# One hybrid decoder layer on one core: branch A's key low parts stored twice per head, so that both score products of branches A and B contract over 128 rows

## The chip, the cores and the metric

The kernel runs on one core of one Trainium2 chip. The metric is device time in microseconds. Three runs of the kernel before took 2040.52, 2048.73 and 2062.89 us; their median is 2048.73. One more execution was recorded by the hardware profiler, and all rows below come from it.

## The reference, cut to what matters

One layer of a decoder with 1024 tokens and 1024 channels: a token mixer of three branches, then a convolutional FFN. All branches read one projection of the normed input. Branch A is dilated sliding-window attention with three (window, dilation) groups of four heads, combined by their softmax denominators. Branch B is grouped-query attention in a window of 128, with sinks. Branch C is stick-breaking attention. A head has 64 channels. The scores of A and B come from blocks of 128 queries against their own block of keys and the one before:

```python
def banded_attention(q, k, v, bias, mask):
    ...
    logits = jnp.einsum('nkgbqd,nkbsd->nkgbqs', qb, kw, preferred_element_type=jnp.float32) * SCALE
    logits = jnp.where(mask, logits + bias[:, :, None], -jnp.inf)
    m = jnp.max(logits, axis=-1)
    p = jnp.exp(logits - m[..., None])
    l = jnp.sum(p, axis=-1)
    num = jnp.einsum('nkgbqs,nkbsd->nkgbqd', p, vw.astype(jnp.float32))
```

The branches' outputs are projected, gated and summed, and an output projection follows. Everything is float32.

## The kernel before, in words

**Precision.** A float32 operand is cut into a high part (type fp32r, which one pass of TensorE carries) and a low part, the rest (`split`, lines 116 to 122). A product is then high by high, high by low and low by high. The large projections are formed from seven half-size products each (`Strassen`); their products are lines 137 and 1333.

**Stages in time.** The pre-norm and the input projections of 27 pairs of column tiles come first, up to about 580 us. Attention of branches A and B follows, up to about 829 us. Then branch C runs with the gated projections of A and B as filler, then C's projection and the output projection, and from about 1130 us the FFN.

**How queries and keys are kept.** After each pair of column tiles `keep_qk` (lines 505 to 534) writes queries and keys to DRAM from a staging tile `hst`, by DMAs on GpSimd's queue. A column tile of 128 channels is two heads. In `q_d` each head has a tile of 128 rows: its high parts on its own 64 rows, its low parts on the other 64. In `k_d` there are four tiles of 128 rows per pair of heads: the high parts of each head, written twice (once on each half of the rows), and the low parts. For branch B and C the low parts of each head are also written twice. For branch A's six key tiles they are written once, both heads under each other, into tile 2 (lines 529 to 531).

**The score products.** `mm_qk` (line 714) forms the scores of one head for one block of queries with two products into the same PSUM columns. Line 717 contracts over all 128 rows: high by high on one half, low queries by high keys on the other. Line 719 adds high queries by low keys and contracts over the 64 rows of that head alone (`r`, rows 0 to 63 for head 0 and 64 to 127 for head 1). Branches A and B both use it. Branch C has its own two products (line 735), both over 128 rows, with key tiles `k` and `kl` per head.

**A step of A or B** (`att_AB`) takes two blocks of 128 queries and two heads. `scores`: eight products into two PSUM tiles `z_ab`, in columns of 128 (own block only) or 256; VectorE adds the bias and finds the row maxima (line 823); ScalarE takes the exponentials (lines 884 and 974; for B also a scaling, line 983). `transposed`: up to eight transposes of the weights on TensorE (line 841, `ps_pT`), copied out by VectorE (line 843). `values`: 128 by 64 products (line 851, `o_ab`). The scores of the next step are issued before the transposes of this one. Branch A has six units (two pairs of heads times three groups, in the order of dilation 4, 16, 1) of four steps each; branch B has four pairs of heads of four steps. One step of A and one of B alternate; B ends after 16 steps and A goes on alone for the last 8.

**Buffers and queues.** SyncE issues the loads, in order. Even units of A have their queries, keys and low keys in pool `ua`, odd ones in a shared tile `HA` and a tile `kl` of pool `ub`; a unit is loaded while the one before it runs. Branch B's values `b_v` have a tile of their own in `ua`; once B is done, the same place takes the low parts of branch C's second head (`c_kl`, two loads). Weights pass through the pool `wa`, tag `raw`, with two buffers. The order on each engine is made by the framework's scheduler from the program's order.

```python
    def mm_qk(z, hh, st, mv, low, ss, ms):
        q, k, kl, r = *low, HR[hh]
        nc.tensor.matmul(z, st[hh][:, ss], mv[hh][:, ms], start=True, stop=False)
        a, b = (q[hh], kl) if st is q else (kl, q[hh])
        nc.tensor.matmul(z, a[r, ss], b[r, ms], start=False, stop=True)
```

Of the kernel before, what the change touches and what calls it, by code (L numbers as in the profile page):

```python
# [18 lines left out]
P = 128  # L19
# [53 lines left out]
def decoder_kernel(ctx, tc, x, rel_bias, attn_pre, w_in, b_gate, sinks, w_br_a, w_br_b, w_br_c,  # L73
# [7 lines left out]
    # Left of SBUF: const, mbuf, hbuf, then what a phase needs; right: wa, b0.  # L81
# [23 lines left out]
    def dram_bc(v):  # L105
        """A row vector in DRAM, read by all partitions."""
        return bass.AP(v.tensor, v.offset, [[0, P], [1, v.shape[-1]]])
# [8 lines left out]
    def split(hi, lo, src, scale=1.0):  # L116
        """src * scale as hi + lo, hi with the bits that one pass of the tensor engine carries."""
# [12 lines left out]
    # float32 products in three passes over exact high and low parts  # L130
# [18 lines left out]
    # Both operands are cut in two along every dimension and the product is formed from seven half-size ones:  # L149
    # S1=A21+A22 S2=S1-A11 S3=A11-A21 S4=A12-S2; T1=B12-B11 T2=B22-T1 T3=B22-B12 T4=B21-T2  # L150
    # P1=A11.B11 P2=A12.B21 P3=S4.B22 P4=A22.T4 P5=S1.T1 P6=S2.T2 P7=S3.T3
    # C11=P1+P2 C12=P1+P6+P5+P3 C21=P1+P6+P7+P4 C22=P1+P6+P7+P5
    # A: the first column tile's channels are the upper rows, the second's the lower. B: channel half, token half.
# [47 lines left out]
    class Strassen:  # L201
# [53 lines left out]
        def products_begin(self, f, ug, uv):  # L255
            """The products in the order in which the operands come; neither needs ug and uv at first."""
# [40 lines left out]
    def operand_build(S, hfs, ks, cols):  # L297
        """Makers of T1, B22 with T2 and T3, and T4 from the halves of h, for the tiles ks and tokens cols; in place of h."""
# [42 lines left out]
    # pairs of column tiles of w_in: queries and keys, values, gates  # L341
# [66 lines left out]
    # Order of the work: n: pre-norm of a token tile; b, c: B11 and B21 of a channel tile (c: from PSUM at once);  # L408
    # x: a channel tile of the second half; t, u, v: T1, then B22 with T2 and T3, then T4 (T, U, V: on the other engine);
    # f: a step of P1 and P2 of a pair; w: weights of the next pair; r: the first pair's other operands.  # L410
# [41 lines left out]
    def init_vectors():  # L452
# [5 lines left out]
        # per-channel vectors, channels on partitions  # L458
# [13 lines left out]
        # bias by distance, reversed, masked distances at NEG; a copy per query row in DRAM  # L472
# [22 lines left out]
    def by_residue(t, dil):  # L495
        """Columns in natural token order, read in residue-major order: token dil * l + r at r * (1024 / dil) + l."""
        return t.rearrange("p (l r) -> p r l", r=dil)
# [7 lines left out]
    def keep_qk(c, u, r):  # L505
# [22 lines left out]
        for part in range(2):  # L528
            if part == 1 and KA <= c < KA + 6:
                nc.gpsimd.dma_start(dst[2], b[:, 1])  # L530
                continue
# [53 lines left out]
    def load_q(dst, c, cols=slice(0, T), eng=nc.sync, which=None):  # L585
        """Two heads' queries: a head's high parts at its rows, low parts at the other's."""
# [3 lines left out]
    def load_k(dst, c, which, cols=slice(0, T), eng=nc.sync):  # L590
        """Keys, high parts twice per head, then low parts."""
        eng.dma_start(dst.bitcast(F32), k_d[KS.index(c), which, :, cols].rearrange("h p t -> p h t"))

    def unit_tiles(odd):
        if odd:
            t = mbuf.tile([P, 4, T], F32R, tag="HA", name="qk")
            q, k, kl = t[:, 0:2], t[:, 2:4], ub.tile([P, 1, T], F32R, tag="kl", name="kl")
        else:
            q = ua.tile([P, 2, T], F32R, tag="q", name="q")
            k3 = ua.tile([P, 3, T], F32R, tag="k", name="k")  # L600
            k, kl = k3[:, 0:2], k3[:, 2:3]
        return dict(k3=None if odd else k3, q=q, k=k, kl=kl, v=(ub if odd else ua).tile([P, NB, P], F32, tag="v", name="v"))
# [4 lines left out]
    def load_A(n):  # L607
# [6 lines left out]
        load_k(u["kl"], KA + 2 * g + p, slice(2, 3))  # L614
        nc.sync.dma_start(u["v"], v_d[VS.index(VA + 2 * g + p)])
        u.update(q=per_head(u["q"]), k=per_head(u["k"]), kl=u["kl"][:, 0])
# [5 lines left out]
    def load_B_qk(p, cols=slice(0, T)):  # L622
        """Both heads of a pair share a key head."""
        if p == 0:
            t = mbuf.tile([P, 4, T], F32R, tag="HD", name="b_qk")
            uB.update(qk=t, q=per_head(t), k=[t[:, 2], t[:, 2]], kl=t[:, 3])
# [7 lines left out]
    def load_C(p, n, t):  # L634
        """Half n of a pair's tokens into t."""
        for hh in range(2):
            load_q(t["q"][hh].unsqueeze(1), QC + p, tok(n), which=hh)
            for i, x in enumerate(("k", "kl")):
                if t[x][hh] is not None:
                    load_k(t[x][hh].unsqueeze(1), KC + p, slice(2 * i + hh, 2 * i + hh + 1), tok(n))  # L640
# [3 lines left out]
    def first_C():  # L644
        u = unit_tiles(0)
        for n in range(2):
            load_q(u["q"][:, :, tok(n)], QC, tok(n))
            load_k(u["k3"][:, :, tok(n)], KC, slice(0, 3), tok(n))
            nc.sync.dma_start(u["v"][:, 4 * n : 4 * n + 4], v_d[VS.index(VC), :, 4 * n : 4 * n + 4])
            uC.setdefault(0, []).append(dict(q=[u["q"][:, hh, tok(n)] for hh in range(2)], k=[u["k"][:, hh, tok(n)] for hh in range(2)],  # L650
                         kl=[u["kl"][:, 0, tok(n)], None], v=u["v"][:, 4 * n : 4 * n + 4]))
# [4 lines left out]
    def last():  # L656
# [5 lines left out]
        uB["v"] = ua.tile([P, NB, P], F32, name="b_v")  # L662
        nc.sync.dma_start(uB["v"], v_d[VS.index(VB)])
# [14 lines left out]
    ub = ph1.enter_context(tc.tile_pool(name="ub", bufs=1))  # L678
    ap = ph1.enter_context(tc.tile_pool(name="att", bufs=2))
# [18 lines left out]
    # weights of the groups as rows, high parts from row 0, low parts from row 32  # L698
# [798 lines left out]
```

## Time and profile before

| what | value |
|---|---|
| median of three runs | 2048.73 us (2040.52 to 2062.89) |
| the profiled execution's own span | 2073.5 us |
| TensorE products, busy | 2000.8 us, 96% of the span |
| VectorE, ScalarE, GpSimd, busy | 1429.1, 1016.7, 290.3 us |
| granted TensorE clock, mean over the span | 0.945 |
| attention of A and B, 580 to 829 us | 249 us, clock 0.62 |

PE is TensorE's products, PEld its weight loads, DVE VectorE, ACT ScalarE, POOL GpSimd and SP SyncE. The granted clock is a share of 2.4 GHz; its two levels here are 1.00 (2.4 GHz) and 0.50 (1.2 GHz). In a timeline a row gives the start, the duration, the engine, the line, the tiles (out<-in), for TensorE the shape (rows contracted * columns of the stationary operand, then the result) and how many instructions were merged. The ends of products are modelled and products overlap, so the distance between two starts tells what one costs better than its duration. The table of windows gives, for each engine, the busy time and the number of instructions in a stretch, then the clock, the share of the DMA engines' time and GB/s.

### The profile page before, as it was taken

What the parts mean: (1) busy time and instruction counts of PE and PEld (TensorE: products, weight loads), DVE (VectorE), ACT (ScalarE), POOL (GpSimd) and SP (SyncE); (2) the same over time, 40 slices, a digit from 0 to 9 for tenths busy, and PEclk for the clock granted to TensorE, in tenths of its full rate; (3) what the DMA queues carried; (4) which work ended last, traced back from release to release, by engine and by line L of the source; (5) the groups of instructions that cost most, each with busy time, mean ns of one, the idle gap of its engine ahead of it and who ended that gap; (6) DMA issues with size and microseconds to landing.
All of it is one profiled execution on the core that took longest, in us unless ns stands there. A gap on an engine that the chain in (4) does not pass through costs nothing.

```text
span 2073.5 us, 24539 instructions
## 1 busy us (share of the span) xinstructions
PE 2000.8 (96%) x8904; PEld 1579.3 (76%) x8904; DVE 1429.1 (69%) x2280; ACT 1016.7 (49%) x1903; POOL 290.3 (14%) x327
## 2 busy tenths in 40 slices
PE   6899999999999999999999999999999999999996
PEld 4788887788866666676687788888888888878874
DVE  7866655354433554879857887877887776488795
ACT  6644333344444653677345554554555454445442
POOL 5121101000110000237525000000000000010131
PEclk9999999999965766999999999999999999999998
DMA  4576534533353424133522322222222225685573
GB/s 144 158 207 192 185 101 144 173 122 122 104 195 102 140 72 129 62 107 123 182 92 82 102 91 82 92 72 82 91 82 81 82 82 190 246 300 188 181 244 122
DMA packets 218777, 277.28 MB, mean 134 GB/s; under 512 B 14543, under 2 KB 145629, under 8 KB 218656
## 3 DMA queue, kind: packets, MB, share of 16 engines
q1 hardware_dynamic: 196400, 198.89, 29.9%
q0 software_dynamic: 22096, 76.76, 10.8%
q8 instruction: 70, 1.15, 0.2%
q14 instruction: 51, 0.42, 0.1%
q10 hardware_dynamic: 160, 0.07, 0.0%
HBM read 204.80 MB, written 74.81 MB: 135 GB/s over the span
## 4 chain that ended last, share of the span: by engine, by line
PE 70%; DVE 10%; issue 9%; DMA 7%; ACT 2%; POOL 1%; SPq 0%; DVEq 0%; POOLq 0%; ACTq 0%
PE st_a L137 24%; PE st_c L137 12%; PE st_b L137 6%; PE e L1333 5%; PE ps_y L137 3%; PE o_ab L851 3%; PE z_ab L719 3%; PE z_ab L717 3%; PE ps_pT L841 3%; PE d L1333 3%; PE ps_b L137 2%; DMA ra<-g_d 2%; DMA rb<-in_w_down_dram 2%; DMA rep_d<-rv_d 1%; DVE sh L120 1%
## 5 line engine op out<-in xcount | busy, mean ns | idle before, releaser
L137 PE MATMUL st_a<-bT,w_hl 128*128 128x512 f32 x2124 | 515.3, 392 | 12.2 <-DVE mixbuf L128 5.2
L137 PEld LDWEIGHTS st_a<-bT,w_hl 128*128 128x128 f32 x2124 | 401.5, 189 | 99.2 <-DVE mixbuf L128 5.6
L118 ACT ACTIVATE w_hl<-w_raw 128x512 fp32r<-128x512 f32 x236 | 147.4, 630 | 308.3 <-PE st_c L137 180.8
L1333 PE MATMUL e<-th,sh 128*128 128x512 f32 x912 | 219.8, 393 | 8.7 <-DVE th L120 5.7
L1333 PEld LDWEIGHTS e<-th,sh 128*128 128x128 f32 x912 | 171.9, 189 | 48.6 <-DVE th L120 10.9
L118 ACT ACTIVATE w_hl<-s 128x512 fp32r<-128x512 f32 x177 | 111.6, 632 | 197.6 <-PE st_a L137 177.7
L120 DVE TENSOR_TENSOR w_hl<-w_raw,w_hl 128x512 fp32r<-128x512 f32 x236 | 165.3, 704 | 55.4 <-ACT w_hl L118 55.2
L137 PE MATMUL st_a<-b,w_hl 128*128 128x512 f32 x708 | 179.4, 399 | 4.7 <-DVE w_hl L120 4.0
L120 DVE TENSOR_TENSOR w_hl<-s,w_hl 128x512 fp32r<-128x512 f32 x177 | 122.8, 695 | 85.1 <-ACT w_hl L118 85.0
L1287 DVE SCALAR_TENSOR_TENSOR ybuf<-ubuf,pvec,ybuf 128x1023 f32<-128x1023 f32 (+1 forms) x128 | 163.8, 1281 | 21.0 <-ACT ybuf L1285 19.9
L137 PE MATMUL st_b<-b,w_hl 128*128 128x512 f32 x708 | 172.3, 391 | 0.2 <-DVE b L120 0.2
L137 PE MATMUL st_c<-bT,w_hl 128*128 128x512 f32 x708 | 170.6, 389 | 0.0
L137 PE MATMUL st_c<-b,w_hl 128*128 128x512 f32 x684 | 164.6, 389 | 0.0
L137 PEld LDWEIGHTS st_a<-b,w_hl 128*128 128x128 f32 x708 | 133.6, 191 | 34.3 <-DVE w_hl L120 4.7
L137 PEld LDWEIGHTS st_b<-b,w_hl 128*128 128x128 f32 x708 | 133.0, 188 | 28.1 <-DVE b L120 0.5
L137 PEld LDWEIGHTS st_c<-bT,w_hl 128*128 128x128 f32 x708 | 133.0, 188 | 27.8 <-ACT w_hl L118 0.2
L137 PEld LDWEIGHTS st_c<-b,w_hl 128*128 128x128 f32 x684 | 128.3, 188 | 26.9 <-ACT ubuf L247 0.2
L1333 PE MATMUL d<-th,sh 128*128 128x512 f32 x432 | 107.5, 393 | 4.4 <-DVE th L120 2.9
L137 PE MATMUL ps_b<-o_hl,wb_hl 128*128 128x512 f32 x384 | 105.2, 399 | 2.5 <-DVE o_hl L120 1.6
L118 ACT ACTIVATE sh<-ra 128x512 fp32r<-128x512 f32 x80 | 50.3, 629 | 106.6 <-PE e L1333 59.5
L843 DVE COPY pT<-ps_pT 128x512 f32<-128x512 f32 (+2 forms) x80 | 46.9, 590 | 79.5 <-PE ps_pT L841 79.2
L1292 POOL DMA_DIRECT2D g_d<-ybuf x32 | 17.1, 535 | 590.6 <-DVE ybuf L1291 590.6
(267 smaller groups left out, 3166.0 us busy)
## 6 DMA issues: line engine op xcount, KB each, us to landing
w_raw<-in_w_up_dram SPq DMA_DIRECT2D x65, 512.0 KB, 4.1
ra<-g_d SPq DMA_DIRECT2D x56, 512.0 KB, 4.6
rb<-in_w_down_dram SPq DMA_DIRECT2D x56, 512.0 KB, 5.0
w_raw<-in_w_in_dram SPq DMA_DIRECT2D x54, 512.0 KB, 5.1
g_d<-ybuf POOLq DMA_DIRECT2D x32, 512.0 KB, 2.9
k_d<-hst POOLq DMA_DIRECT2D x30, 512.0 KB, 8.8
gate_d<-mixbuf POOLq DMA_DIRECT2D x24, 512.0 KB, 4.4
gate<-gate_d SPq DMA_DIRECT2D x48, 256.0 KB, 3.3
```

Source lines behind the costliest of these rows:

```text
L118: nc.scalar.activation(hi, src, AF.Copy, scale=scale)
L120: nc.vector.tensor_tensor(lo, src, hi.bitcast(F32), op=ALU.subtract)
L137: nc.tensor.matmul(ps, st(a, k), mv(b, k), start=start and n == 0, stop=stop and n == 3 * nk - 1, **kw)
L717: nc.tensor.matmul(z, st[hh][:, ss], mv[hh][:, ms], start=True, stop=False)
L719: nc.tensor.matmul(z, a[r, ss], b[r, ms], start=False, stop=True)
L841: nc.tensor.transpose(ps[:, n, :], prs[hh][:, b, c * P : c * P + P], ident)
L843: nc.vector.tensor_copy(pT[:, : len(slots), :], ps[:, : len(slots), :])
L851: nc.tensor.matmul(o[HR[hh], (i % 4) * P : (i % 4) * P + P], v[:, i - (nch - 1) + c, vcol(hh) : vcol(hh) + 64], pTs[hh][:, n, :], start=(c ...
L1287: nc.vector.scalar_tensor_tensor(y[:, d:], src[:, : T - d], cw[2 - d][:, c : c + 1], y[:, d:], op0=ALU.mult, op1=ALU.add)
L1292: nc.gpsimd.dma_start(g_d[f * P : f * P + P, :], ys[0])
L1333: nc.tensor.matmul(banks[m], sh[:, a, m * P : m * P + P], th[:, b], start=start and f0, stop=kk == NK - 2 and e == 1 and n == 2, skip_grou ...
```

## The change

Branch A's low key parts are now written like all others: twice per head, into tiles 2 and 3 of `k_d`. The tiles `kl` grow from one to two per unit, and the second product of every score contracts over all 128 rows, with the low keys of the head on both halves. It so adds low queries by low keys too. To make room, branch B's values move from their own tile in `ua` to one of the two `raw` buffers of `wa`, and their load moves with them. C's first pair now gets the low parts of both heads with the others, so the two late loads `c_kl` go. Comments and docstrings were removed as well.

```diff
         dst = k_d[KS.index(c)]
         for part in range(2):
-            if part == 1 and KA <= c < KA + 6:
-                nc.gpsimd.dma_start(dst[2], b[:, 1])
-                continue
             for hh in range(2):
                 nc.gpsimd.dma_start(dst[2 * part + hh].rearrange("(a d) t -> d a t", a=2),
                                     b[HR[hh], part].unsqueeze(1).broadcast_to([64, 2, T]))
...
-            q, k, kl = t[:, 0:2], t[:, 2:4], ub.tile([P, 1, T], F32R, tag="kl", name="kl")
+            q, k, kl = t[:, 0:2], t[:, 2:4], ub.tile([P, 2, T], F32R, tag="kl", name="kl")
...
-            k3 = ua.tile([P, 3, T], F32R, tag="k", name="k")
-            k, kl = k3[:, 0:2], k3[:, 2:3]
+            k4 = ua.tile([P, 4, T], F32R, tag="k", name="k")
+            k, kl = k4[:, 0:2], k4[:, 2:4]
...
-        load_k(u["kl"], KA + 2 * g + p, slice(2, 3))
+        load_k(u["kl"], KA + 2 * g + p, slice(2, 4))
...
-            uB.update(qk=t, q=per_head(t), k=[t[:, 2], t[:, 2]], kl=t[:, 3])
+            uB.update(qk=t, q=per_head(t), k=[t[:, 2], t[:, 2]], kl=[t[:, 3], t[:, 3]])
...
-            load_k(u["k3"][:, :, tok(n)], KC, slice(0, 3), tok(n))
+            for i, x in enumerate(("k", "kl")):
+                load_k(u[x][:, :, tok(n)], KC, slice(2 * i, 2 * i + 2), tok(n))
...
-        uB["v"] = ua.tile([P, NB, P], F32, name="b_v")
-        nc.sync.dma_start(uB["v"], v_d[VS.index(VB)])
...
     ub = ph1.enter_context(tc.tile_pool(name="ub", bufs=1))
+    uB["v"] = wa.tile([P, NB, P], F32, tag="raw", name="b_v")
+    nc.sync.dma_start(uB["v"], v_d[VS.index(VB)])
...
-    def mm_qk(z, hh, st, mv, low, ss, ms):
-        q, k, kl, r = *low, HR[hh]
-        nc.tensor.matmul(z, st[hh][:, ss], mv[hh][:, ms], start=True, stop=False)
-        a, b = (q[hh], kl) if st is q else (kl, q[hh])
-        nc.tensor.matmul(z, a[r, ss], b[r, ms], start=False, stop=True)
+    def mm_qk(z, q, k, kl, ss, ms):
+        nc.tensor.matmul(z, q[:, ss], k[:, ms], start=True, stop=False)
+        nc.tensor.matmul(z, q[:, ss], kl[:, ms], start=False, stop=True)
...
-            kl1 = ua.tile([P, T], F32R, tag="b_v", name="c_kl1")
-            for i in range(2):
-                uC[0][i]["kl"][1] = kl1[:, tok(i)]
-                load_k(uC[0][i]["kl"][1].unsqueeze(1), KC, slice(3, 4), tok(i))
```

On TensorE the instructions of the attention stretch stand in the same order as before, row for row; only their line numbers and the height of the second product differ. From the first products of branch C on, C's products and the filler are dealt a little differently.

GpSimd's queue in the input projections, where the queries and keys of the first two pairs of column tiles are written (`q_d`, `k_d`; + and - mark the change):

```order
 L523 DMA q_d<-hst 64x2x1024
 L525 DMA q_d<-hst 64x1024
-L533 DMA k_d<-hst 64x2x1024 x2
-L530 DMA k_d<-hst 128x1024
+L530 DMA k_d<-hst 64x2x1024 x4
 L523 DMA q_d<-hst 64x2x1024
 L525 DMA q_d<-hst 64x1024 x2
```

Two transfers of high parts and one of low parts have become four transfers of the same size.

SyncE's queue before, from the last weights of the input projections to the loads of A's first unit (`bias`, `q`, `k`, `v`) and B's values (`b_v`); `wb_raw` are the weights of B's projection:

```order
L156 DMA w_raw<-in_w_in_dram 128x8x128 x13
L1022 DMA wb_raw<-in_w_br_b_dram 128x4x128 x5
L580 DMA bias<-rep_d 128x2x256
L588 DMA q<-q_d 128x2x1024
L592 DMA k<-k_d 128x2x1024
L592 DMA k<-k_d 128x1024
L615 DMA v<-v_d 128x1024
L580 DMA bias<-rep_d 128x2x256
L663 DMA b_v<-v_d 128x1024
```

The same place of the changed kernel:

```order
L156 DMA w_raw<-in_w_in_dram 128x8x128 x13
L675 DMA b_v<-v_d 128x1024
L1017 DMA wb_raw<-in_w_br_b_dram 128x4x128 x4
L577 DMA bias<-rep_d 128x2x256
L585 DMA q<-q_d 128x2x1024
L589 DMA k<-k_d 128x2x1024 x2
L612 DMA v<-v_d 128x1024
L577 DMA bias<-rep_d 128x2x256
```

B's values have moved ahead of the weights of B's projection, of which one fewer is loaded there, and the low keys of A's first unit are twice as many.

SyncE's queue before, at the loads of A's last unit (`qk`, `kl`, `v`), behind the statistics `stn` of the unit two before it, and of C's first pair (`q`, `k`):

```order
L592 DMA qk<-k_d 128x2x1024
L912 DMA stn<-sd_5790 128x8x4
L592 DMA kl<-k_d 128x1024
L592 DMA c_kl_6158<-k_d 128x512 x2
L615 DMA v<-v_d 128x1024
L588 DMA q<-q_d 128x2x512
L592 DMA k<-k_d 128x3x512
```

The same place of the changed kernel:

```order
L589 DMA qk<-k_d 128x2x1024
L907 DMA stn<-sd_5796 128x8x4
L589 DMA kl<-k_d 128x2x1024
L1017 DMA wb_raw<-in_w_br_b_dram 128x4x128
L612 DMA v<-v_d 128x1024
L585 DMA q<-q_d 128x2x512
L589 DMA k<-k_d 128x2x512 x2
```

Where two loads into the place of `b_v` stood, a load of weights now waits for the buffer of `b_v`.

## Rows read from the trace of the kernel before

**Rows 1.** The page's first line: the profiled execution's own time.

```profile
span 2073.5 us, 24539 instructions
```

**Rows 2.** Table of windows: from:to, length, busy us per engine, clock, DMA share, GB/s.

```profile
580.00:829.00 249.00, 248.18 (x1081) 166.91 (x1079) 115.31 (x499) 121.76 (x434) 11.96 (x20) 0.62 0.36 117
...
770.00:829.00 59.00, 58.49 (x253) 39.33 (x252) 27.70 (x101) 25.72 (x97) 2.07 (x3) 0.60 0.50 153
...
850.00:975.00 125.00, 123.30 (x638) 86.22 (x637) 109.02 (x163) 90.01 (x172) 55.95 (x42) 1.00 0.33 108
100.00:260.00 160.00, 160.00 (x715) 132.43 (x714) 103.20 (x137) 74.29 (x108) 30.01 (x52) 1.00 0.66 198
```

**Rows 3.** The same table, three stretches of 4 us in the attention stretch.

```profile
584.00:588.00 4.00, 4.00 (x9) 2.29 (x8) 1.45 (x9) 2.49 (x11) 0.00 (x0) 0.50 1.02 405
640.00:644.00 4.00, 4.00 (x25) 2.89 (x25) 2.40 (x9) 0.75 (x4) 0.00 (x0) 0.50 0.02 4
644.00:648.00 4.00, 4.00 (x24) 2.73 (x20) 1.68 (x6) 3.64 (x11) 0.00 (x0) 0.91 0.40 131
```

**Rows 4.** TensorE's timeline at the low clock: pairs of score products.

```profile
590.13 0.47 PE L717 MATMUL z_ab<-k,q 128*128 128x128 f32 x1
590.53 0.47 PE L719 MATMUL z_ab<-k,q 64*128 64x128 f32 x1
590.93 0.58 PE L717 MATMUL z_ab<-k,q 128*128 128x256 f32 x1
591.44 0.58 PE L719 MATMUL z_ab<-k,q 64*128 64x256 f32 x1
```

**Rows 5.** TensorE's timeline at the high clock: score products and transposes.

```profile
718.88 0.38 PE L719 MATMUL z_ab<-k,q 64*128 64x256 f32 x1
719.19 0.87 PE L841 MATMUL ps_pT<-ident,pr 128*128 128x128 f32 x6
719.82 0.31 PE L717 MATMUL z_ab<-b_qk 128*128 128x128 f32 x1
...
721.18 0.33 PE L717 MATMUL z_ab<-b_qk 128*128 128x128 f32 x1
721.44 0.32 PE L719 MATMUL z_ab<-b_qk 64*128 64x128 f32 x1
```

**Rows 6.** TensorE's timeline: value products at the high clock, transposes at the low.

```profile
714.29 1.09 PE L851 MATMUL o_ab<-pT,b_v 128*64 128x128 f32 x14
715.31 0.38 PE L717 MATMUL z_ab<-k,q 128*128 128x256 f32 x1
...
819.69 1.54 PE L841 MATMUL ps_pT<-ident,pr 128*128 128x128 f32 x6
820.88 0.56 PE L717 MATMUL z_ab<-qk 128*128 128x256 f32 x1
```

**Rows 7.** TensorE's timeline at the high clock: branch C's score products.

```profile
871.90 0.62 PE L735 MATMUL z_c<-q,k 128*128 128x256 f32 x3
872.36 0.28 PE L735 MATMUL z_c<-q,c_kl 128*128 128x256 f32 x1
872.48 0.34 PE L735 MATMUL z_c<-q,k 128*128 128x128 f32 x2
```

**Rows 8.** Groups by shape, VectorE, 580 to 829 us: the reductions of the scores.

```profile
L823 DVE CUSTOM_DVE_ANT_0 s_ab<-z_ab,bias 128x256 f32<-128x256 f32 x100 | 39.6, 416 | 16.4 <-PE z_ab L719 12.1 <-ACT pr L983 3.0 <-ACT pr L974 1.1
...
L823 DVE CUSTOM_DVE_ANT_0 s_ab<-z_ab,bias 128x128 f32<-128x128 f32 x60 | 16.4, 287 | 30.9 <-PE z_ab L719 28.0 <-ACT pr L983 1.7 <-ACT pr L974 0.7
```

**Rows 9.** Table of windows for one tile alone: transposes (`ps_pT`), then value products (`o_ab`).

```profile
580.00:829.00 249.00, 62.73 (x252) 38.56 (x252) 44.80 (x77) 0.62 0.36 117
...
580.00:829.00 249.00, 68.33 (x488) 47.18 (x488) 5.52 (x8) 15.11 (x27) 0.62 0.36 117
```

**Rows 10.** DMA issues: count, KB each, median us from issue to landing.

```profile
k_d<-hst POOLq DMA_DIRECT2D x30, 512.0 KB, 8.8
...
kl<-k_d SPq DMA_DIRECT2D x3, 512.0 KB, 4.0
```

More of the change, by code (lines that the diff above doesn't have):

```diff
@@ L596, in unit_tiles @@
             t = mbuf.tile([P, 4, T], F32R, tag="HA", name="qk")
-            q, k, kl = t[:, 0:2], t[:, 2:4], ub.tile([P, 1, T], F32R, tag="kl", name="kl")
+            q, k, kl = t[:, 0:2], t[:, 2:4], ub.tile([P, 2, T], F32R, tag="kl", name="kl")
         else:
             q = ua.tile([P, 2, T], F32R, tag="q", name="q")
-            k3 = ua.tile([P, 3, T], F32R, tag="k", name="k")
-            k, kl = k3[:, 0:2], k3[:, 2:3]
-        return dict(k3=None if odd else k3, q=q, k=k, kl=kl, v=(ub if odd else ua).tile([P, NB, P], F32, tag="v", name="v"))
+            k4 = ua.tile([P, 4, T], F32R, tag="k", name="k")
+            k, kl = k4[:, 0:2], k4[:, 2:4]
+        return dict(q=q, k=k, kl=kl, v=(ub if odd else ua).tile([P, NB, P], F32, tag="v", name="v"))
     def per_head(t):
@@ L613, in load_A @@
         load_k(u["k"], KA + 2 * g + p, slice(0, 2))
-        load_k(u["kl"], KA + 2 * g + p, slice(2, 3))
+        load_k(u["kl"], KA + 2 * g + p, slice(2, 4))
         nc.sync.dma_start(u["v"], v_d[VS.index(VA + 2 * g + p)])
-        u.update(q=per_head(u["q"]), k=per_head(u["k"]), kl=u["kl"][:, 0])
+        u.update({x: per_head(u[x]) for x in ("q", "k", "kl")})
         return u
@@ L638, in load_C @@
             for i, x in enumerate(("k", "kl")):
-                if t[x][hh] is not None:
-                    load_k(t[x][hh].unsqueeze(1), KC + p, slice(2 * i + hh, 2 * i + hh + 1), tok(n))
+                load_k(t[x][hh].unsqueeze(1), KC + p, slice(2 * i + hh, 2 * i + hh + 1), tok(n))
         nc.sync.dma_start(t["v"], v_d[VS.index(VC + p), :, 4 * n : 4 * n + 4])
@@ L647, in first_C @@
             load_q(u["q"][:, :, tok(n)], QC, tok(n))
-            load_k(u["k3"][:, :, tok(n)], KC, slice(0, 3), tok(n))
+            for i, x in enumerate(("k", "kl")):
+                load_k(u[x][:, :, tok(n)], KC, slice(2 * i, 2 * i + 2), tok(n))
             nc.sync.dma_start(u["v"][:, 4 * n : 4 * n + 4], v_d[VS.index(VC), :, 4 * n : 4 * n + 4])
-            uC.setdefault(0, []).append(dict(q=[u["q"][:, hh, tok(n)] for hh in range(2)], k=[u["k"][:, hh, tok(n)] for hh in range(2)],
-                         kl=[u["kl"][:, 0, tok(n)], None], v=u["v"][:, 4 * n : 4 * n + 4]))
+            half = {x: [u[x][:, hh, tok(n)] for hh in range(2)] for x in ("q", "k", "kl")}
+            uC.setdefault(0, []).append(dict(v=u["v"][:, 4 * n : 4 * n + 4], **half))
     proj.post = keep
@@ L817, in scores @@
                     i, w = i0 + b, ws[b]
-                    mm_qk(z[:, b, :w], hh, q, k, (q, k, kl), slice(i * P, i * P + P), slice((i + 1) * P - w, (i + 1) * P))
+                    mm_qk(z[:, b, :w], q[hh], k[hh], kl[hh], slice(i * P, i * P + P), slice((i + 1) * P - w, (i + 1) * P))
                 s = ap.tile([P, 2, 2 * P], F32, tag="s", name="s_ab", bufs=3)
```

## Prediction

> **What bounds the kernel now.** I read the table of the span in slices first, then windows, then the timeline of TensorE. The profiled span is 2073.5 us [rows 1]. Its granted TensorE clock is at the full level nearly everywhere except between about 580 and 829 us, where it averages 0.62 [rows 2]. That stretch is the attention of branches A and B, and I call it the attention stretch. TensorE is busy for 248.18 of its 249.00 us there, while VectorE works 115.31 and ScalarE 121.76 [rows 2]. So TensorE sets the pace, and nothing else ends last. The reader should see that "busy" does not mean "at work at its speed": the clock is 0.50 while TensorE is busy without a gap [rows 3].
>
> Why it is slow there stands in the timeline. Score products come in pairs: the first contracts over 128 rows, the second over 64. Their starts lie 0.40 us apart for 128 columns and 0.51 for 256 at the low clock (1.2 GHz) [rows 4], and 0.26 and 0.31 at the high one (2.4 GHz) [rows 5]. Products that follow one of their own shape go much faster. Six transposes take 0.63 us at the high clock, or 0.105 each [rows 5], and 1.19 at the low one, or 0.20 each [rows 6]. The nearest relatives of the score products are branch C's. They are already two products per head over all 128 rows, added into the same PSUM columns: four of them with 256 columns take 0.58 us, and the last step is 0.12 [rows 7]. So it is the change of shape, not the addition into one place, that costs time: the weight load of the next product does not slip under the current one.
>
> **The change, part by part.** *Second product over 128 rows.* The count and the columns of the products stay, and so does TensorE's order in this stretch. What goes is the change of shape on either side of 160 second products: 100 with 256 columns and 60 with 128, since VectorE reduces each once [rows 8]. Counted in the program's order, about 290 of these 320 changes go; the others touch a value product (128 by 64), which keeps its own shape. The price of one change is the spacing now minus the spacing without it. At the low clock it is 0.51 - 0.24 = 0.27 for 256 columns (0.24 is twice branch C's 0.12, an estimate) and 0.40 - 0.20 = 0.20 for 128. At the high clock it is 0.31 - 0.12 = 0.19 and 0.26 - 0.105 = 0.15. A mean of 0.62 between 0.5 and 1.0 means that 24% of the stretch's time is at the high clock; work passes faster there, so I put one third of the pairs in it. Two changes per pair then give 67 x 0.54 + 33 x 0.38 + 40 x 0.40 + 20 x 0.30 = 36 + 13 + 16 + 6 = 71 us, and 0.9 of that is **64 us** with the clock as it is now.
>
> *The clock.* It falls with the score products and comes back after runs of value products in one shape: 640 to 644 holds 25 products, and the next window shows 0.91 [rows 3]. In the projections (100 to 260 us) and in branch C (850 to 975 us), where products mostly keep one shape, it is 1.00 throughout [rows 2]. With score products back to back I expect 1.00 here too. TensorE's work at the high clock is then: scores 200 x 0.12 + 120 x 0.105 = 37; transposes 252 x 0.105 = 26 [rows 5, 9]; value products 488 x 0.073 = 36, from 14 in 1.02 us [rows 6, 9]; some 110 changes of shape that stay, at about 0.13 = 15; and about 4 for the few products that weight branch A's groups. That is 118 us, about as much as VectorE's 115 and ScalarE's 122, so no engine bounds the stretch alone and it cannot fall below 122.
>
> How closely can three equal engines overlap? The nearest row is branch C's 125 us, where VectorE reaches 109.02, or 87%, with independent work to fill gaps [rows 2]. Up to 770 us two independent streams run (A and B). ScalarE's share of that is 121.76 - 25.72 = 96, and I take it at 80%: 120 us. After 770 branch A is alone, one step ahead of itself, with 27.70 us of VectorE [rows 2]. I take that at 65%: 42 us. The stretch comes to **162 us instead of 249, a gain of 87**. Its bounds are 140 (122 at 87%) and 185 (249 - 64).
>
> *Key low parts kept twice.* Six key tiles are written by four transfers instead of three: six more of 512 KB on GpSimd's queue, behind which the same pair's later writes wait. They land within 8.8 us [rows 10], and a pair of column tiles has some 20 us. TensorE is busy for all of 100 to 260 us at a DMA share of 0.66 [rows 2], which hides them. Without that cover, six pairs would each lose at most one landing, 53 us; I take 0.
>
> *Loads.* The low-part load of each of six units doubles to 1024 KB. Now 512 KB takes 4.0 us to land [rows 10], so I bound the delay of each by nothing and by another 4.0. They are issued about a unit ahead, and a unit still lasts over 15 us. I take 0 for the first five and up to 4 us where branch A is alone. Branch B's values move ahead of branch A's first loads on SyncE's queue and occupy one of the two weight buffers until B ends. Fewer of B's projection weights are loaded ahead, but these are needed only after 830 us. The one that waits for B's end stands on the queue where a load of branch C's low parts waited for the same release, so unit 5's values and C's first loads behind it wait no longer than now. C's own order shifts by a few products; I give that plus or minus 3 us.
>
> A rule of the Trainium skill speaks against the change. TensorE: Matmul & The Clock Gate, in Part 3 (Packing small matmuls), says that products on different row groups run concurrently. Here the two heads' second products do sit on different halves of the rows. By that rule the second products would cost almost nothing, and 128 rows would add their full time. The rows disagree: what follows a 64-row product starts 0.40 us later, like what follows a 128-row one, since a full-height product stands between any two [rows 4].
>
> **Against the runs shown.** The profiled span is 24.8 us above the median of 2048.7. If that is the price of being profiled, the result is 2048.7 - 87 = 1962. If instead the profiled stretch stayed at the low clock for longer than in the runs (which differ by 22 us among themselves), it is 2073.5 - 87 = 1986. I take the middle, **1974 us**, 3.6% faster.
>
> **The rivals.** (1) *The clock does not rise.* Shape changes at value products remain, and waits for VectorE and ScalarE add gaps that TensorE does not have now. At an unchanged mix the gain is 64. With the low clock throughout TensorE needs 200 x 0.24 + 120 x 0.20 + 252 x 0.20 + 488 x 0.146 + 110 x 0.2 + 6 = 222, a gain of 27. The times are 1985 to 2022, middle 2000. (2) *Near perfect overlap*: 140 us in the stretch, 109 gained, 1940 to 1950. (3) *The change doesn't do what it says*: the price is that of a pair adding into one place, not of the rows; then nothing changes, 2049. Branch C's rows speak against it [rows 7]. (4) *Slower by late loads*: each unit waits for its doubled load, on the one queue that also waits for branch A's statistics. It ends slower by 1% only if the waits eat the gain and 20 us more: over 107 us, 21 at each of five unit boundaries, against a price of 4.0; about 2070. (5) *Slower by lost concurrency*, the rule above: 160 second products x 0.12 to 0.24 = 19 to 38 us, so 2068 to 2087. It would need a pair that starts almost together, and the rows show none [rows 4, 5].
>
> **How the numbers follow.** Chances: forecast 0.64, (1) 0.18, (2) 0.06, (3) 0.06, (4) 0.04, (5) 0.02. The forecast's own range is 1950 to 1995, from a stretch of 145 to 180 us and either reading of the 24.8. The 80% range adds most of (1) and the edge of (2): 1945 to 2012. About 1% is what a measurement of this kernel can tell from no change. Faster by more than that: 0.64 + 0.18 + 0.06 = 0.88; within 1%: 0.06; slower: 0.06.
>
> **What would show it.** Score products 0.11 to 0.13 us apart in one tile; a clock of 0.95 or more from 580 us to branch C; the stretch near 162 us with ScalarE the busiest, at about 75%; projections as before. It is wrong if spacings stay at 0.4 to 0.5 (3), if the clock is still near 0.6 (1), if TensorE waits for loads at unit boundaries (4), or if the engines wait on each other so long that no one exceeds 65%.

## The result, and the profile after

The changed kernel takes **1961.48 us** (median of 4 runs, 1958.97 to 1967.42) against 2053.35 us before (4 runs, 2040.52 to 2062.89). The ratio is 0.958, with a 95% interval of 0.953 to 0.964: 4.2% faster. The forecast was 1974 us in a range of 1945 to 2012.

The page's first line of the changed kernel, to be held against [rows 1]:

```profile
span 1957.5 us, 24553 instructions
```

The table of windows of the changed kernel (from:to, length, busy us per engine with the count of instructions, granted TensorE clock, DMA share, GB/s): the whole attention stretch, its two parts (A and B together, A alone), 4 us near its start, and the projections. They answer to [rows 2, 3].

```profile
576.00:712.00 136.00, 129.38 (x1089) 101.48 (x1087) 111.96 (x502) 118.75 (x436) 12.03 (x20) 1.00 0.64 212
576.00:678.00 102.00, 97.11 (x830) 77.17 (x829) 84.25 (x398) 93.26 (x340) 9.95 (x17) 1.00 0.64 219
678.00:712.00 34.00, 32.27 (x260) 24.31 (x260) 27.70 (x105) 25.49 (x97) 2.07 (x3) 1.00 0.63 191
584.00:588.00 4.00, 3.56 (x26) 2.44 (x27) 2.83 (x15) 4.00 (x16) 2.11 (x5) 1.00 1.03 387
100.00:260.00 160.00, 160.00 (x715) 132.53 (x714) 102.87 (x137) 73.66 (x108) 33.29 (x58) 1.00 0.78 214
```

The stretch that took 249 us takes 136, at a clock of 1.00 instead of 0.62, with nearly the same work of VectorE (112 us, before 115) and ScalarE (119, before 122). In the window from 584 to 588 us TensorE now starts 26 instructions where it started 9. But only score products stood there before, and transposes and value products are among them now; the timeline below compares like with like. The projections are untouched (715 instructions in 160 us, as before), although the DMA share there rose from 0.66 to 0.78. The stretch gives 113 of the 116 us by which the two spans differ; most of the rest lies ahead of it.

TensorE's timeline of the changed kernel (start, us, engine, line, operation), beside [rows 4, 5]: a pair that follows value products, then the middle of a tile.

```profile
589.75 0.87 PE L846 MATMUL o_ab<-pT,v 128*64 128x128 f32 x10
590.55 0.33 PE L713 MATMUL z_ab<-k,q 128*128 128x128 f32 x1
590.72 0.27 PE L714 MATMUL z_ab<-k,q 128*128 128x128 f32 x1
...
592.11 0.28 PE L714 MATMUL z_ab<-b_qk 128*128 128x256 f32 x1
592.23 0.28 PE L713 MATMUL z_ab<-b_qk 128*128 128x256 f32 x1
592.35 0.28 PE L714 MATMUL z_ab<-b_qk 128*128 128x256 f32 x1
```

Inside a tile the products of 256 columns start 0.12 us apart, where they stood at 0.31 (high clock) and 0.51 (low). The step right behind another kind of work is longer (0.17 here).

What the doubled storage became: DMA issues of the whole execution (count, KB each, median us to landing), beside [rows 10], and all that TensorE waited for in the stretch (line, releaser, us in total, times, longest).

```profile
k_d<-hst POOLq DMA_DIRECT2D x36, 512.0 KB, 7.4
...
kl<-k_d SPq DMA_DIRECT2D x3, 1024.0 KB, 11.5
```

```profile
PE z_ab L713 <- DVE nm L818: 2.8, 5, 1.0
PE z_ab L713 <- DVE st L818: 1.7, 3, 0.9
PE ps_pT L836 <- ACT pr L978: 0.8, 3, 0.4
PE ps_pT L836 <- DVE pT L838: 0.5, 2, 0.3
PE o_ab L846 <- ACT pr L879: 0.2, 1, 0.2
PE ps_pT L836 <- ACT pr L879: 0.2, 1, 0.2
```

The low-part loads of the odd units (`kl`) take 11.5 us to land, nearly three times the 4.0 of before, but no load is among TensorE's waits. (In a second profiled execution of the changed kernel there is one, of 0.3 us.)

### The profile page after: what moved, and what is told of

It reads as the page before. It is cut to its first block, busy times and chain, and to the rows that moved or that the text cites. A ratio compares the mean times of both kernels' runs of the same rounds, so it can differ in the third digit from the quotient of the medians.

```text
span 1957.5 us, 24553 instructions
## 1 busy us (share of the span) xinstructions
PE 1881.5 (96%) x8904; PEld 1514.4 (77%) x8904; DVE 1421.5 (73%) x2280; ACT 1011.5 (52%) x1903; POOL 292.5 (15%) x333
## 4 chain that ended last, share of the span: by engine, by line
PE 68%; DVE 11%; issue 9%; DMA 7%; ACT 3%; POOL 1%; SPq 0%; DVEq 0%; POOLq 0%; ACTq 0%
PE st_a L137 27%; PE st_c L137 13%; PE st_b L137 6%; PE e L1324 5%; PE ps_y L137 4%; PE d L1324 3%; PE ps_b L137 2%; DMA ra<-g_d 2%; PE o_ab L846 2%; PE ps_pT L836 1%; DMA rb<-in_w_down_dram 1%; DVE sh L120 1%; DMA rep_d<-rv_d 1%; DVE th L120 1%; PE z_ab L713 1%
## 5 line engine op out<-in xcount | busy, mean ns | idle before, releaser
L1324 PEld LDWEIGHTS d<-th,sh 128*128 128x128 f32 x432 | 82.4, 191 | 23.1 <-DVE th L120 3.5
```

Of the source, the lines that this page charges most:

```text
L1324: nc.tensor.matmul(banks[m], sh[:, a, m * P : m * P + P], th[:, b], start=start and f0, stop=kk == NK - 2 and e == 1 and n == 2, skip_grou ...
```

## Experiments

The theory is that of the prediction: a change in the number of rows between neighbouring products costs time at once, and it also takes the clock down. The storage, loads and the number of rows themselves cost nothing. The texts set off below were put on record before each run.

**The storage without the rows, and the rows without the storage.** First the changed kernel with the second product back at a head's 64 rows:

```diff
-        nc.tensor.matmul(z, q[:, ss], kl[:, ms], start=False, stop=True)
+        nc.tensor.matmul(z, q[r, ss], kl[r, ms], start=False, stop=True)
```

> The changed kernel with its new storage (low parts of branch A's keys written and loaded twice, branch B's values in the weight buffers), but with the second score product back at 64 rows, a head's own. Theory (the gain is the change of row height between products and the clock that follows it; the storage costs nothing): the time of the kernel before, ratio 0.99 to 1.01, and the stretch from the first score product to branch C's first again 235 to 250 us at a clock near 0.6. Rival (part of the gain comes from the storage or the moved loads): 10 us or more faster than before. Rival (the storage costs something that the products' gain hides): 10 us or more slower.

Then the kernel before with nothing but the rows changed:

```diff
-        nc.tensor.matmul(z, a[r, ss], b[r, ms], start=False, stop=True)
+        nc.tensor.matmul(z, a[:, ss], b[:, ms], start=False, stop=True)
```

> The kernel before with nothing changed but the rows of the second score product: 128 instead of 64, on the old storage, so that in branch A it takes in the other head's low parts as well (its output is not the reference's in branch A). Theory: all of the gain, 1955 to 1970 us, ratio 0.953 to 0.963, clock 1.00 from 580 us on, score products of one tile 0.11 to 0.13 us apart. Rival (the storage and loads give a part of the gain): it stays 10 us or more above the changed kernel. Rival (the new storage costs something): 5 us or more below the changed kernel's 1961.

Measured: 2048.4 us, ratio to the kernel before 1.004 (0.999 to 1.008), and 1960.85 us, ratio 0.960 (0.954 to 0.966), the changed kernel's time within 1 us. The rows of the score product are the whole gain and the storage costs nothing that can be measured. The windows of the first, the stretch and two pieces of it, then the stretch of the second:

```profile
580.00:797.00 217.00, 215.44 (x1084) 146.24 (x1082) 115.33 (x500) 121.54 (x435) 11.67 (x20) 0.75 0.43 147
602.00:631.00 29.00, 29.00 (x194) 20.48 (x195) 18.02 (x84) 20.87 (x76) 1.42 (x2) 1.00 0.52 179
634.00:675.00 41.00, 41.00 (x163) 28.32 (x164) 16.11 (x76) 16.90 (x63) 1.36 (x2) 0.50 0.38 123
```

```profile
581.00:716.00 135.00, 128.59 (x1075) 102.13 (x1074) 110.38 (x499) 117.66 (x431) 11.53 (x19) 0.97 0.60 194
```

The first has another lesson. It has the products of the kernel before, yet its stretch took 217 us at a clock of 0.75, not 249 at 0.62, and so missed the expected 235 to 250. Within it 29 us ran at the high clock with 194 instructions, and 41 us at the low one with 163. How long such a stretch stays at the low level differs from one execution to the next. The times go with it: beside these experiments the kernel before ran anywhere from 2018 us (granted clock 0.972 over the whole) to 2073 us (0.944), and the changed one, run again in them, only from 1960.3 to 1964.7 (0.985 to 0.989).

An estimate from these rows: at the low level a score product of 256 columns takes 0.51/0.31 = 1.65 times as long. By that factor both stretches, 249 us with 24% at the high level and 217 us with half, come to about 174 us if all of it ran at the high level. So the clock alone can explain the difference between them. Of the 113 us by which the profiled stretch became shorter, some 75 would then be the clock and some 38 the changes themselves.

**The same products in another order.** In the kernel before, each tile's two 128-row products first and then its two 64-row ones. `mm_qk` yields after each product; two sums are then open in one bank at a time, and the results are not the reference's:

```diff
-                    mm_qk(z[:, b, :w], hh, q, k, (q, k, kl), slice(i * P, i * P + P), slice((i + 1) * P - w, (i + 1) * P))
+                    pairs_.append(mm_qk(z[:, b, :w], hh, q, k, (q, k, kl), slice(i * P, i * P + P), slice((i + 1) * P - w, (i + 1) * P)))
+                for _ in range(2):
+                    for x in pairs_:
+                        next(x)
```

> The kernel before with the same products on the same rows, but in each tile of scores both blocks' 128-row products first and then both 64-row products: the changes of row height fall from 320 to about 160. Theory (a change of height has a price, the number of rows has none): at the old clock half of the direct gain, about 35 us, so about 2015; if the clock comes back as well, the stretch is bound by TensorE at 118 plus 160 changes of 0.17, 145 us, and the time comes to 1965 to 1985. Rival (it is the 64 rows themselves that are slow, or two products that add into one place): nothing changes, 2040 to 2060.

Measured: 1990.5 us, ratio 0.975 (0.969 to 0.980). No product lost or gained a row, and 52 us of the median (2042.6 in these runs) went. So it is the change that costs. The rival, slow 64-row products, falls. That two products add into one place is not the cost either: in the run before this one they still do, back to back, at the changed kernel's time.

**Two pairs in five.** The changed kernel with branch B's second products at 64 rows:

```diff
-        nc.tensor.matmul(z, q[:, ss], kl[:, ms], start=False, stop=True)
+        nc.tensor.matmul(z, q[r, ss], kl[r, ms], start=False, stop=True)
...
-                    mm_qk(z[:, b, :w], q[hh], k[hh], kl[hh], slice(i * P, i * P + P), slice((i + 1) * P - w, (i + 1) * P))
+                    mm_qk(z[:, b, :w], q[hh], k[hh], kl[hh], HR[hh] if u is uB else slice(0, P), slice(i * P, i * P + P), slice((i + 1) * P - w, (i + 1) * P))
```

> The changed kernel with branch B's second products back at 64 rows and branch A's left at 128: 64 of the 160 pairs change height again. Theory with a clock that follows the share of such changes: where A and B run together TensorE needs 64 times 2 changes of 0.15 to 0.19 more, 19 to 24 us at the high clock, so 1975 to 1985 if the clock holds at 1.00; if it falls to 0.5 there, the joint part becomes about 150 us instead of 100, 2000 to 2015. Where A is alone (the last 41 us) nothing changes. Rival (the changes cost only at the low clock, so that a few of them are free): 1961 as the changed kernel.

Measured: 1982.4 us, ratio 0.971 (0.966 to 0.976): as the theory has it when the clock holds. The stretches of the two runs, reordered first:

```profile
576.00:744.00 168.00, 165.73 (x1090) 119.19 (x1089) 114.00 (x501) 121.31 (x436) 12.07 (x20) 0.89 0.52 176
```

```profile
577.00:735.00 158.00, 154.82 (x1096) 113.20 (x1096) 113.61 (x503) 120.54 (x436) 12.00 (x20) 0.95 0.55 187
```

The clock does not follow the changes in proportion: with 160 of 320 left it is back at 0.89, with 128 left at 0.95. The reordered kernel lies between its two forecasts (1965 to 1985 with the clock back, 2015 without).

**The price by itself.** Blocks of products behind the end of the kernel before, with nothing else running. Each kind names its rows, the columns of its stationary operand and its bank (used where the block's second number is 1):

```diff
+    FU, UP, LO = (full, P, 0), (up_, P, 0), (lo_, P, 1)
+    block(240, 0, FU)
+    block(240, 0, FU, UP)
+    block(240, 0, FU)
+    block(160, 0, UP)
+    block(160, 1, UP, LO)
+    block(160, 1, FU, (full, P, 1))
+    block(160, 0, FU, (full, 64, 0))
+    block(160, 0, FU, FU, UP, UP)
```

> The kernel before, with eight blocks of score-like products of 256 columns behind the end of its work, one after the other on TensorE with nothing else running; what they compute is not used. The time of the whole says nothing, the spacing inside the blocks does, at the high clock. Blocks: (1) 240 products over 128 rows; (2) 240, by turns over 128 and over the first 64 rows; (3) as 1; (4) 160 over the first 64 rows; (5) 160, by turns over the first and the last 64 rows, into two banks; (6) 160 over 128 rows, by turns into two banks; (7) 160 over 128 rows, by turns with 128 and with 64 stationary columns; (8) 160, two over 128 rows and two over 64 by turns. Theory (the change of height costs, the number of rows does not): 1, 3, 4 and 6 at 0.12 us, 2 at 0.31, 8 at 0.24, 7 near 0.21, and the clock goes to the low level in block 2 and is high in blocks 3 and 4. For block 5 there are three answers: 0.06 if products on different halves of the rows run at the same time, as TensorE: Matmul & The Clock Gate, Part 3 (Packing small matmuls), of the Trainium skill has it; 0.12 if a change of half costs nothing and brings nothing; 0.31 if it costs what a change of height does. Rival to the theory (64 rows are slow in themselves, or the bank is what counts): 4 at 0.2 or more, or 6 unlike 1.

Windows inside the blocks, in order: 1 at its start and then later, 2 just after its start, 2, 3, 4, 5, 6, 7, 8 after its start, 8. Length over count is the spacing.

```profile
2043.30:2046.50 3.20, 3.19 (x15) 3.19 (x16) 1.41 (x2) 0.00 (x0) 0.12 (x1) 0.50 0.56 216
2050.00:2074.00 24.00, 24.00 (x202) 24.00 (x202) 0.00 (x0) 0.00 (x0) 0.00 (x0) 1.00 0.01 1
2075.00:2079.00 4.00, 4.00 (x14) 2.33 (x13) 0.00 (x0) 0.00 (x0) 0.00 (x0) 1.00 0.00 0
2085.00:2190.00 105.00, 105.00 (x207) 58.92 (x206) 0.00 (x0) 0.00 (x0) 0.00 (x0) 0.50 0.00 0
2200.00:2224.00 24.00, 24.00 (x202) 24.00 (x201) 0.00 (x0) 0.00 (x0) 0.00 (x0) 1.00 0.01 1
2226.00:2243.00 17.00, 17.00 (x144) 17.00 (x143) 0.00 (x0) 0.00 (x0) 0.00 (x0) 1.00 0.00 1
2244.00:2253.00 9.00, 9.00 (x155) 9.00 (x154) 0.00 (x0) 0.00 (x0) 0.00 (x0) 1.00 0.01 2
2254.00:2273.00 19.00, 19.00 (x160) 19.00 (x160) 0.00 (x0) 0.00 (x0) 0.00 (x0) 1.00 0.00 1
2274.00:2291.00 17.00, 17.00 (x148) 17.00 (x147) 0.00 (x0) 0.00 (x0) 0.00 (x0) 1.00 0.01 2
2292.50:2297.50 5.00, 5.00 (x25) 3.53 (x24) 0.00 (x0) 0.00 (x0) 0.00 (x0) 1.00 0.00 0
2300.00:2344.00 44.00, 44.00 (x122) 30.33 (x122) 0.00 (x0) 0.00 (x0) 0.00 (x0) 0.50 0.00 0
```

All full-height: 0.119, and 0.213 in the first 3 us, which are still at the low clock. All 64 rows: 0.118. By turns: 0.31 from start to start while the clock is still high (of the 14 in that window the outer two lie in it only in part), and then 0.507 (105/207) at the clock of 0.50, in which the block stays until full-height products return. These are the kernel's own 0.31 and 0.51 [rows 4, 5]. A change therefore costs 0.19 us at the high clock. In two-and-two order the mean is about 0.2 (5/25), where 0.24 was expected, and again the clock goes to 0.50. The reordered kernel has that order in its tiles and kept 0.89, with transposes and value products between them. In blocks 2 and 8 the weight loads (second column: 58.92 of 105, 30.33 of 44) no longer fill the time: a load does not slip under a product of another height. Banks and a narrower output cost nothing here (blocks 6, 7: 0.119, 0.115); for block 7 about 0.21 was expected.

Block 5 was the open one: products by turns on the two halves of the rows come every 0.058 us, two at a time. The kernel before could not profit because a full-height product stood between any two. The rule that spoke against the change (the Trainium skill, TensorE: Matmul & The Clock Gate, Part 3, Packing small matmuls: products on separate parts of the array run at the same time) holds here, then: 0.058 against 0.118. The Trainium skill, TensorEngine Tiling (Array Packing), Key Properties, says that changing the tiling mode drains the engine and that changing only the tile does not; blocks 2 and 5 agree, and add the price, while block 7, which alternates 128 and 64 stationary columns, shows none (0.115).

**A second set of blocks** behind the changed kernel, for value-like products and for mixtures. Here a kind names rows, stationary columns, bank and output columns; FU, UP and LO are as above, with 256 columns:

```diff
+    TR, CL, CR = (full, full, 0, 128), (full, up_, 0, 128), (full, lo_, 0, 128)
+    block(160, CL, CR)
+    block(160, CL)
+    ...
+    block(160, TR, CL)
+    block(160, FU, CL)
+    block(160, FU, TR)
+    ...
+    block(160, FU, FU, FU, FU, UP, LO, UP, LO)
+    ...
+    block(160, FU, FU, FU, FU, FU, FU, FU, UP)
```

> The changed kernel with eleven blocks of products behind the end of its work, nothing else running; what they compute is not used and the time of the whole says nothing. 256-column products are of the score products' type, 128-column ones plain float32 as transposes and value products are. Blocks (240 products in the first, 160 in each other): (1) 128 rows, 256 columns; (2) value-like products by turns into the lower and the upper half of the output partitions; (3) into the lower half alone; (4) 128 by 128, 128 columns; (5) by turns 4's and 3's; (6) by turns 1's and 3's; (7) by turns 1's and 4's; (8) as 1; (9) four of 1, then four of 64 rows by turns on the first and the last half of the rows; (10) as 1; (11) seven of 1 and one of 64 rows. It asks what the 0.20 us around value products is, whether 64-row products of two heads on two halves would pay (block 9), and whether one change of height in four products is enough to bring the clock down (block 11). Theory (a change of the used rows or of the output half costs, a change of type does not): 2 at 0.06 if halves of the output run together; 5 and 6 at 0.11 to 0.12 as in the run before; 9 at 0.19 less what two at a time save, a mean of 0.12 to 0.15; 11 a mean of 0.16 with the clock high. Rival (the change of type is what costs at value products): 6 and 7 at 0.2 or more, 5 not.

Windows inside blocks 2, 3, 5, 6, 7, 9 and 11 (a plain float32 product stands as two instructions in the trace):

```profile
1985.00:2001.00 16.00, 16.00 (x299) 16.00 (x295) 0.00 (x0) 0.00 (x0) 0.00 (x0) 1.00 0.01 2
2002.00:2036.00 34.00, 34.00 (x314) 34.00 (x313) 0.00 (x0) 0.00 (x0) 0.00 (x0) 1.00 0.01 1
2073.00:2134.00 61.00, 61.00 (x314) 38.19 (x314) 0.00 (x0) 0.00 (x0) 0.00 (x0) 1.00 0.00 1
2136.00:2188.00 52.00, 52.00 (x232) 29.01 (x231) 0.00 (x0) 0.00 (x0) 0.00 (x0) 1.00 0.00 1
2190.00:2216.00 26.00, 26.00 (x232) 26.00 (x231) 0.00 (x0) 0.00 (x0) 0.00 (x0) 1.00 0.00 1
2236.00:2257.00 21.00, 21.00 (x155) 15.86 (x153) 0.00 (x0) 0.00 (x0) 0.00 (x0) 1.00 0.00 1
2277.00:2303.00 26.00, 26.00 (x159) 21.01 (x158) 0.00 (x0) 0.00 (x0) 0.00 (x0) 1.00 0.00 1
```

Two halves of the output run together as well (0.054 against 0.108 for one half alone). Block 5 misses both answers on record. Plain float32 products of 128 and of 64 output columns by turns do cost a change (0.194 per instruction, where each kind alone has 0.11), while a change of type alone (block 7, 0.112) is free. Block 6, score-like and value-like products by turns, is what the changed kernel still has around its value products. One score-like product and the two instructions of a value-like one take 0.67 us there (52 us for 232 instructions), against 0.34 when each kind runs alone, so a change is 0.17. Why the narrower output was free in the first set, with products of the other type, stays open. Block 9 shows that keeping 64 rows and running two heads at a time would not have paid in groups of four: 8 products in 8 x 0.135 = 1.08 us, against 8 x 0.12 = 0.96 over 128 rows. Block 11, with one 64-row product in eight, has a mean of 0.164, as expected, and the clock stays at 1.00.

**What bounds the stretch now.** ScalarE is at 91% while A and B run together, so the theory was ScalarE and the rival TensorE. Less work on TensorE, without the second product:

> The changed kernel without the second score product (160 of them left out, so the keys' low parts do not enter branches A and B); storage and loads stay. It asks whether TensorE still sets the pace of the stretch, which takes 131 us from the first score product to branch C's first. Theory (ScalarE does now: 115.92 of these 131 us): the stretch comes down by at most 6 us, to 1955 to 1961 us. Rival (TensorE still does): it comes down by the spacing of 160 products, 0.12 to 0.16 each, 19 to 25 us, to 1936 to 1943.

Less on ScalarE, branch B's scaling left out:

> The changed kernel without branch B's scaling of the weights by the reciprocal row sums (64 ScalarE instructions of 0.49 us, 26.5 us, left out; B's output is not normalised). It takes work from ScalarE and gives it to nobody. Theory (ScalarE sets the pace where A and B run together, 93 of 101 us): that part comes down to what VectorE's 84 us allow, 88 to 93 us, so 8 to 13 us faster than the changed kernel, 1948 to 1953 us. Rival (each unit is bound by the chain through its own steps, and the load of no engine matters much): less than 4 us.

Measured: 1960.2 us (1953.1 to 1961.6) and 1958.5 us (1956.1 to 1964.0), neither clear of the changed kernel's own 1958.97 to 1967.42. In the first run the ScalarE theory's 1955 to 1961 came true and the TensorE rival fell. In the second the ScalarE theory's 1948 to 1953 fell and its rival, less than 4 us, came true. The changed kernel's stretch, then that of the first run and its joint part:

```profile
577.00:708.00 131.00, 124.42 (x1050) 97.58 (x1049) 108.73 (x490) 115.92 (x426) 11.49 (x19) 1.00 0.62 212
...
580.00:710.00 130.00, 117.42 (x889) 84.33 (x888) 107.44 (x489) 114.41 (x421) 11.82 (x20) 0.91 0.66 218
580.00:678.00 98.00, 89.10 (x697) 64.62 (x695) 83.03 (x395) 92.19 (x338) 9.75 (x17) 0.93 0.69 236
```

The joint part of the second run:

```profile
576.00:672.00 96.00, 92.88 (x796) 75.59 (x795) 79.34 (x378) 69.85 (x277) 9.14 (x16) 0.98 0.67 235
```

With 160 products fewer, TensorE's busy time fell by only 7 us (124 to 117), at a clock of 0.91 instead of 1.00, so that this run took less off TensorE than was meant. ScalarE still works 92 of 98 us in the joint part. With ScalarE down to 70 us, TensorE is busy for 93 of 96. Whichever is relieved, the other is there. Relieving both at once was not run, so that the two share the bound is argued, not shown, and the second run's rival, a chain through the steps of each unit, stays open.

**Three attempts at a better balance.** Half of B's scaling on GpSimd (`nc.gpsimd.tensor_scalar(pr, pr, l[...], None, op0=ALU.mult)` for one head):

> The changed kernel with branch B's scaling of the weights by the reciprocal row sums moved from ScalarE to GpSimd for one head of two: 32 instructions of 0.49 us, 13 of ScalarE's 116 us in the stretch. GpSimd works 11 us of 131 there. Theory (ScalarE sets the pace where A and B run together): 3 to 8 us faster, 1953 to 1958. Rival (GpSimd needs 0.83 us for such a tile and the transposes wait for it, or it slows VectorE): no gain, or up to 10 us slower, 1961 to 1971.

B's 36 steps spread over A's 54 (`range(2 if m == 0 else m % 3 != 1)`; a step here is one `yield` of the program, nine to a unit):

> The changed kernel with branch B's 36 steps spread over all 54 steps of branch A (two in three) instead of one with each, so that B ends with A and A is alone nowhere. Theory (ScalarE is at 92% while both run and at 68% in the 41 us in which A is alone): at 92% throughout the stretch becomes about 8 us shorter, 1953 us. Rival (branch C's first tiles and branch B's output weights wait for buffers that B now frees 36 us later): no gain or slower, 1961 to 1985.

Branch A's output copies on VectorE (`nc.vector.tensor_copy(num[n], o)`, and the same for the strided ones), beside the changed kernel itself:

> The changed kernel with branch A's copies of its outputs out of PSUM (19 instructions of 0.6 us, 10.5 us in the stretch) moved from ScalarE to VectorE. In the part where A and B run together that makes 86 and 91 of 101 us instead of 93 and 84. Theory (the busiest engine sets the pace at 92%): 0 to 3 us faster, 1958 to 1961. Rival (VectorE's reductions and copies out of PSUM, for which TensorE waits, come later): 2 to 8 us slower.

> The changed kernel itself once more, beside the run above on the same chip: 1958 to 1966 us.

Measured: 1965.05, 1962.8, 1964.3, and 1961.8 for the changed kernel again. None gains; each time the median lies where the rival had put it. The GpSimd group, and TensorE's longest wait in that run:

```profile
L981 POOL TENSOR_SCALAR pr<-pr,l 128x256 f32<-128x256 f32 (+1 forms) x32 | 28.0, 882 | 43.7 <-DVE l L974 32.2 <-ACT pr L879 10.8 <-PE o_ab L846 0.5
```

```profile
PE ps_pT L836 <- POOL pr L981: 4.3, 5, 2.9
```

GpSimd needs 0.88 us where ScalarE needed 0.49, and the transposes wait for it. The clock has a part as well: over the stretch it was 0.93 in this run and 0.95 with the copies on VectorE, but 1.00 in both profiled executions of the changed kernel. How much of the loss that makes is not shown. No version here that does all the work beats the changed kernel.

## Why the prediction was right, and where a term was off

- **The cause** (a change of height, not the rows and not the pair adding into one place) was right. Rows alone give everything, while the pairs still add into one place; the order alone gives 52 us, and 64-row products among themselves run at 0.118. Rival 3 falls.
- **The price of a change** was right at the high clock: 0.31 - 0.12 = 0.19, as in the blocks. At the low one it was 0.27 and should be about 0.30, since full-height products stand at 0.213 there (block 1 at its start), not at twice 0.12. The 0.13 for a change that stays, around value products, had no row; blocks 5 and 6 give 0.17.
- **The clock** came back to 1.00, as forecast. Rival 1 falls, and more clearly than its chance of 0.18: even half of the changes leave it near 0.9. Whether waits bring the clock down, as that rival thought, stays open: the stretch stood at 0.91 with 12 us of TensorE's waits (no second product), but also at 0.96 with 4 us (no scaling), and at 1.00 with 6 us in the changed kernel.
- **The stretch** is the mis-sized term: 162 us forecast, 136 measured. The joint part took 102 instead of 120 (ScalarE at 91%, not 80%), branch A alone 34 instead of 42 (VectorE at 81%, not 65%). The nearest row, branch C's 87%, was read and then discounted without a row for the discount. Over the whole stretch ScalarE reached 118.75 of 136 us, which is 87%. The forecast had ScalarE as the busiest engine; it is TensorE, whose work was summed to 118 us and which is busy for 129. In the stretch it was rival 2 (140 us) that came true; its total of 1940 to 1950 did not, since it was counted from the runs' median.
- **Against the runs**, the 24.8 us were split in the middle, and should not have been. Being profiled costs next to nothing: the changed kernel's profiled execution took 1959.31 us. The profiled execution of before had simply stayed at the low clock for longer than most. By that reading the forecast was 2073.5 - 87 = 1986; with 113 instead of 87 it gives 1960.5. Two errors, 26 us too little gain and 12 us from the split, partly cancelled, which is why the total was only 12.5 us off. That is luck. The forecast's own range was also narrower than its terms: a stretch of 145 to 180 us and either reading give 1945 to 2005, not 1950 to 1995.
- **Writes and loads** at nothing: right. The doubled loads land later (11.5 us), which is more than the bound of 8, but in the profiled execution no product waits for them, and the storage alone has a ratio of 1.004. The bound was also read from the odd units alone: the low parts of the even ones, loaded into tile `k`, took 7.4 us before. Rival 4 falls.
- **Lost concurrency** (rival 5): the ability is real (0.058 us apart in block 5), the kernel never used it, as the prediction read from the timeline.

## What to carry to other kernels

A TensorE that is busy without a gap may be spending much of that time on changes between product shapes: divide the length of a window by its count of instructions and compare it with a window of uniform products. Before splitting a contraction over fewer rows to save storage or work, see what stands next to it in order; an alternating 64-row product costs more than the 128-row one that replaces it. And take the overlap of several engines from the nearest row as it stands, unless a row supports the discount: here 87% came back as 87%, though one case does not make that a rule.

## What had not been expected

- TensorE reports no idle time while changes of height hold it at the low clock (block 2: busy 105 of 105 us at 0.50). That was expected; not expected was that the two-and-two order goes to 0.50 in block 8 and stays at 0.89 in the reordered kernel.
- Products of 128 and of 64 output columns by turns pay 0.17 us per change in plain float32 and nothing as score-like products, where both had been expected the other way round.
- Taking 26 us of work off ScalarE brought 3 us, where 8 to 13 were forecast.
- Two executions of the same products spent 217 and 249 us in the same stretch, at clocks of 0.75 and 0.62. A kernel that moves between the two levels has a wide spread (2018 to 2073), and a single profile of it is a poor base for a sum.
- Products on different halves of the rows, or of the output, start in pairs: 0.058 and 0.054 us on average, half of a single stream's spacing. On record that was one answer of three, and the kernel before could not have shown it.
